# Prompt tokens normalized as rows with a broadcast row of norm weights, first loads in another order, the sample's rstd spread through DRAM

## The chip, the cores and the metric

The kernel runs on one core of a Trainium2 chip. The metric is the device time of one execution in microseconds (us); a lower one is better. The profile is that of one execution, and times in it count from the start of its span.

## The reference

An encoder layer is applied to two batches with the same weights: a prompt of 512 tokens and a sample of 1024 tokens, each token a row of 1024 float32 numbers. Cut to what matters:

```python
def encoder_layer(x, norm_g, w_in, ...):
    h = rmsnorm(x, norm_g)                 # x * rsqrt(mean(x*x) + EPS) * g, row by row
    proj = h @ w_in
    qa, ka, va, za, qb, kb, vb, zb, ga, gb = jnp.split(proj, ...)
    # branch A: 2-D neighbourhood attention, 8 heads; q and k normed by head
    oa = neighbourhood_attention(qa, ka, va, rpb_a) * silu(za)
    # branch B: windowed grouped-query attention with a sink logit and a T5 bias
    ob = window_gqa_attention(qb, kb, vb, t5_table, sink_b) * silu(zb)
    merged = sigmoid(ga) * (oa @ w_o_a) + sigmoid(gb) * (ob @ w_o_b)
    return x + merged @ w_out
```

`norm_g` holds one weight per column, and the factor rsqrt(...), called rstd here, is one number per token.

## The kernel before

Tokens are taken in tiles of 128: four for the prompt, eight for the sample. Everything that a matmul reads is split into a high and a low part (`hh` and `hl` for the normalized tokens, `whi` and `wlo` for weights), and each product is three matmuls: high by high, high by low, low by high. ScalarE writes the high part with a copy, and VectorE or GpSimd subtracts it from the source for the low part. The matmuls want `hh` and `hl` with columns on the partitions and tokens along the row, so tokens have to be transposed.

The work goes in four stages: the prompt's attention, the prompt's dense products, the sample's attention, the sample's dense products. An attention stage has six groups (A0 to A3, B0, B1). For each group four weight pieces of 128x768 are loaded and split (`att_weights`, L568 to L583), and for each token tile 24 matmuls make q, k and v (`project`, L732). The q and k of a tile are then normed (L748 to L784), transposed (L829), and split (L850 to L869); blocks of queries are scored (L902), biased (L937), put through the exponential (L946), scaled (L970 to L978), transposed (L994) and multiplied with v (L1031). The bias of a head is the difference of a mask and a table (L666), where the table comes by way of DRAM: `expand` (L405) writes rows of it out there, and L653 reads them back. Three dense products are taken ahead of their stage as fillers (`fill_gates`, L1430, loads at L1440, tiles `fr`, `fh`, `fl`, PSUM tag `d`).

The order of instructions is made by the class `Flow` (L136). Every operation is recorded with a priority, the engines it may run on, and what it comes behind; `run` (L202) then plays the program through with durations and lags of its own and writes each engine's instructions in the order that comes out. A predecessor in an `after` list is obeyed in that play; on the chip an instruction waits for the data and buffers that it uses.

The prompt's tokens are normalized in `norm_tile` (L504). `rstd` (L432) loads a tile (L438), ScalarE sums its squares (L441), and GpSimd makes the power of -0.5 (L445, L449). TensorE transposes the raw tile in eight blocks (L514). The rstd stands one per partition, while the transposed tokens need it along the row on all partitions, so `spread_rstd` (L454) has ScalarE scale an identity by it (`diag`, L458), TensorE multiply that with a matrix of ones (L463), and ScalarE copy the result out of PSUM (`rb`, L468). `scaled_parts` (L472) then multiplies, 128 columns of the model at a time, the transposed block with the norm weight of its partition (`gx`) and with `rb` (L484), ScalarE copies `hh` (L491) and VectorE or GpSimd subtracts `hl` (L496).

The sample's tokens come transposed from DRAM (`norm_pair`, L537, during the prompt's dense stage). Their rstd is made earlier, tile by tile in the prompt's attention (L1585), with the same `spread_rstd`, into one `rb` of 128x1024.

Loads are issued by SP, one after another in its order. The first stage is opened at L1577; `START` (L32) and `NORM` (L35) are the priorities of the tile loads and of the norms, `FIRST_POOL` (L34) names the weight pieces of the first group whose low part GpSimd has to take, and `setup` (L591) and `expand_ops` (L585) load small tables and expand the bias tables.

## Time and profile before

| what | value |
|---|---|
| time, median of 3 runs (lowest to highest) | 1159.51 us (1157.9 to 1161.04) |
| the profiled execution's own time | 1160.63 us |
| its span, first to last instruction | 1158.8 us |
| TensorE matmuls busy | 1139.2 us |
| VectorE, ScalarE, GpSimd busy | 854.4, 652.2, 325.0 us |
| mean granted TensorE clock | 0.998 |
| bytes moved by DMA | 159.34 MB, mean 138 GB/s |

In the lines of the profile PE is TensorE's matmuls, PEld its weight loads, DVE VectorE, ACT ScalarE, POOL GpSimd and SPq the transfers that SP issues. A line of the timeline has its start in us, its length in us, the engine, the line of the kernel, the operation, what it writes and reads, and in brackets how long the engine stood idle before it and what ended that. A short row of instructions of one kind is one line, with its count. Matmuls overlap: the length of one is the time to its end, and the step from one start to the next is what it costs.

### The profile page before, as it was taken

The numbers are of one execution on the slowest core, as the hardware profiler recorded it, in microseconds if no ns is written. First come the engines' busy times: TensorE is split into PE (matmuls) and PEld (weight loads), VectorE is DVE, ScalarE is ACT, GpSimd is POOL, SyncE is SP. The second block draws the span as 40 slices with busy tenths as digits, with TensorE's granted clock in tenths as the row PEclk, the third lists the DMA queues.
The fourth block names the chain that finished last, engine by engine and source line by source line (L and its number), as shares of the span: only waits on it lengthen the run. The fifth ranks groups of instructions, "written<-read, shape, count | busy, mean of one in ns | idle before, by whom it ended". The sixth has DMA issues, their size and how long they took to land.

```text
span 1158.8 us, 18608 instructions
## 1 busy us (share of the span) xinstructions
PE 1139.2 (98%) x6154; PEld 986.5 (85%) x6154; DVE 854.4 (74%) x1964; ACT 652.2 (56%) x1492; POOL 325.0 (28%) x442
## 2 busy tenths in 40 slices
PE   7999999999999999999999999999999999999998
PEld 6899888888887899999999888888888888788887
DVE  6877888486766468787878888875878555497984
ACT  6966987554434246565768888864534344343320
POOL 4664454100000042434326534440122110031110
PEclk9999999999999999999999999999999999999999
DMA  9842433687786422121212122125767334664072
GB/s 301 302 141 78 130 108 93 152 267 230 232 262 223 151 86 66 33 64 29 71 40 89 38 64 65 37 64 173 245 171 211 115 121 139 216 225 130 28 218 91
DMA packets 124545, 159.34 MB, mean 138 GB/s; under 512 B 28273, under 2 KB 66929, under 8 KB 124449
## 3 DMA queue, kind: packets, MB, share of 16 engines
q1 hardware_dynamic: 124448, 158.16, 44.7%
q8 instruction: 48, 0.79, 0.3%
q14 instruction: 49, 0.39, 0.1%
HBM read 121.40 MB, written 41.44 MB: 141 GB/s over the span
## 4 chain that ended last, share of the span: by engine, by line
PE 84%; ACT 3%; DVE 3%; DMA 2%; issue 1%; POOL 1%; ACTq 0%; DVEq 0%
PE p L732 21%; PE x L1249 9%; PE x L1250 9%; PE x L1248 9%; PE x L1031 4%; PE x L902 4%; PE x L994 4%; PE p L1249 4%; PE p L1248 4%; PE p L1250 4%; PE d L1248 4%; PE d L1250 4%; PE d L1249 4%; PE x L829 1%; DMA ot<-u_d 1%
## 5 line engine op out<-in xcount | busy, mean ns | idle before, releaser
L732 PE MATMUL p<-wlo,hh 128*128 128x384 f32 x384 | 132.0, 344 | 1.6 <-POOL wlo L580 1.6
L732 PE MATMUL p<-whi,hh 128*128 128x384 f32 x384 | 132.9, 347 | 0.6 <-ACT whi L575 0.6
L732 PE MATMUL p<-whi,hl 128*128 128x384 f32 x384 | 132.9, 346 | 0.0
L946 ACT ACTIVATE sb<-sb,mx 128x384 f32<-128x384 f32 (+1 forms) x192 | 107.8, 566 | 21.1 <-DVE mx L937 20.8
L1136 POOL TENSOR_TENSOR wlo<-raw,whi 128x512 fp32r<-128x512 f32 x26 | 37.6, 1445 | 270.9 <-ACT whi L1131 270.8
L1131 ACT ACTIVATE whi<-raw 128x512 fp32r<-128x512 f32 (+1 forms) x140 | 81.2, 590 | 55.1 <-PE x L1249 25.1
L732 PE MATMUL p<-whi,hb 128*128 128x384 f32 x384 | 109.0, 349 | 0.2
L1248 PE MATMUL x<-hh,whi 128*128 128x512 f32 x264 | 102.8, 389 | 1.7 <-ACT hh L1131 1.7
L1249 PE MATMUL x<-hl,whi 128*128 128x512 f32 x264 | 102.8, 389 | 0.2 <-DVE hl L1136 0.2
L1250 PE MATMUL x<-hh,wlo 128*128 128x512 f32 x264 | 102.7, 389 | 0.0
L1005 DVE TENSOR_TENSOR pp<-x,pp 128x512 fp32r<-128x512 f32 (+1 forms) x136 | 82.5, 637 | 22.0 <-ACT pp L1000 21.7
L1136 DVE TENSOR_TENSOR wlo<-raw,whi 128x512 fp32r<-128x512 f32 (+1 forms) x114 | 72.2, 648 | 30.3 <-ACT whi L1131 30.1
L1249 PE MATMUL x<-T,whi 128*128 128x512 f32 x224 | 87.4, 390 | 0.4 <-DVE T L1136 0.2
L1248 PE MATMUL x<-T,whi 128*128 128x512 f32 x224 | 87.3, 390 | 0.1
L1250 PE MATMUL x<-T,wlo 128*128 128x512 f32 x224 | 87.2, 389 | 0.0
L1000 ACT ACTIVATE pp<-x 128x512 fp32r<-128x512 f32 (+1 forms) x136 | 70.8, 562 | 20.8 <-PE x L994 20.0
L767 POOL TENSOR_TENSOR rs_r<-rs_v,mhalf 128x4 f32<-128x4 f32 (+1 forms) x72 | 79.9, 1110 | 5.6
L1031 PE MATMUL x<-pp,v 128*128 128x256 f32 (+1 forms) x368 | 78.5, 325 | 1.4 <-DVE pp L1005 1.4
L732 PEld LDWEIGHTS p<-whi,hh 128*128 128x128 f32 x384 | 72.8, 190 | 1.9 <-ACT whi L575 0.9
L732 PEld LDWEIGHTS p<-wlo,hh 128*128 128x128 f32 x384 | 72.7, 189 | 2.0 <-POOL wlo L580 1.8
L732 PEld LDWEIGHTS p<-whi,hl 128*128 128x128 f32 x384 | 72.7, 189 | 1.8 <-issue 1.5
L732 PEld LDWEIGHTS p<-whi,hb 128*128 128x128 f32 x384 | 69.1, 189 | 3.5 <-ACT hb L633 0.8
(343 smaller groups left out, 2982.3 us busy)
## 6 DMA issues: line engine op xcount, KB each, us to landing
raw<-in_w_g_dram SPq DMA_DIRECT2D x76, 256.0 KB
w<-in_w_att_dram SPq DMA_DIRECT2D x48, 384.0 KB
ot<-o_d SPq DMA_DIRECT2D x36, 256.0 KB
g_d<-C SPq DMA_DIRECT2D x34, 256.0 KB
raw<-in_w_z_dram SPq DMA_DIRECT2D x32, 256.0 KB
raw<-in_w_out_dram SPq DMA_DIRECT2D x32, 256.0 KB
C<-g_d SPq DMA_DIRECT2D x24, 256.0 KB
out_dram<-C SPq DMA_DIRECT2D x23, 256.0 KB
```

Of the source, the lines that this page charges most:

```text
L732: pe.matmul(ps.t[:, :GW], part[u](k), mv.t[:, c], start=k == 0 and m == 0, stop=k == KC - 1 and m == 2,)
L767: lambda e: nc.gpsimd.tensor_tensor(r.t[:, :nn], rv.t[:, :nn], mhalf[:, :nn], op=ALU.pow),
L902: pe.matmul(pss[2 * pair + i].t[:, :width], q.t[rows, u, at : at + P], kv[:, tiles[0] : tiles[-1] + 1 : step], start=n == 0, stop=n == 2,)
L946: act.activation(sb.t[:, :width], sb.t[:, :width], AF.Exp, bias=mx.t[:, i : i + 1], scale=-1.0, accum_out=sm.t[:, i : i + 1],)
L1000: lambda e, pt=pt, pp=pp, nn=nn: act.activation(pp.t[:, 0, :nn], pt.t[:, :nn], AF.Copy),
L1005: lambda e, pt=pt, pp=pp, nn=nn: dve.tensor_tensor(pp.t[:, 1, :nn], pt.t[:, :nn], pp.t[:, 0, :nn].bitcast(F32), op=ALU.subtract),
L1031: pe.matmul(out(), v.t[:, vs], mv(), start=first, stop=last)
L1131: (("act", ACT_(n)),), lambda e: act.activation(hi(), src(), AF.Copy), prio,
L1136: lambda e: engines[e].tensor_tensor(lo(), src(), hi().bitcast(F32), op=ALU.subtract), prio,
L1248: pe.matmul(out, hi.t[:, cs], mh(), start=first and k == 0, stop=False)
L1249: pe.matmul(out, hi.t[:, cs], ml(), start=False, stop=False)
L1250: pe.matmul(out, lo.t[:, cs], mh(), start=False, stop=last and k == len(ws) - 1)
```

## The change

*The norm of the prompt.* The tile is no longer transposed raw. A row of all 1024 norm weights is loaded onto every partition in two halves of 512 columns (`gb`, L1595 of the new code). VectorE multiplies the tile as it lies, tokens on partitions, with its rstd (one per partition) and with that row, 256 columns at a time for tile 0 and 512 for the others (L497). TensorE transposes the products (L507), ScalarE copies `hh` out of PSUM (L512), and VectorE subtracts `hl` out of PSUM (L517). `diag`, the matrix of ones, the L463 matmul and the copy to `rb` are gone for the prompt.

*The sample's rstd.* The eight tiles' rstd are kept as columns of one 128x8 tile `r_s`, which SP writes to DRAM in token order and reads back as a row on all partitions (L1612, L1613), once, in place of eight rounds over ScalarE, TensorE and ScalarE.

*Loads.* Their order at the start is another. Two of the first group's four weight pieces land in a buffer that a bias tile uses later (`place`), so that all four can be asked for at once. Predecessors are given to the loads of tiles 2 and 3, of the bias tables, of the small tables, of the second group's weights, of the sample's tiles and of the fillers' weights (`begun` holds the first matmul of a group and tile). `FIRST_POOL` is empty, so GpSimd is no longer forced on any weight piece.

The diff, cut to its core:

```diff
-FIRST_POOL = (0, 2)
+FIRST_POOL = ()
...
-    def rstd(pool, x, t, prio, load_prio, bufs, after=()):
+    def rstd(pool, x, t, prio, load_prio, bufs, after=(), load_after=(), out=None):
...
+        r = out or val([P, 1], F32, "nr", bufs)
+        rv = lambda: r.t[:, t : t + 1] if out else r.t
+        f.dma(lambda: nc.sync.dma_start(xt.t, x[t * P : (t + 1) * P, :]), 524288, load_prio, new=[xt], after=load_after)
...
-    def spread_rstd(pool, r, t, rb, prio):
...
-    def norm_tile(pool, x, hh, hl, t, prio, load_prio, after=()):
+    def norm_tile(pool, x, gb, gb_ops, hh, hl, t, prio, load_prio, after=(), load_after=()):
+
+        xt, r = rstd(pool, x, t, prio, load_prio, 4, after, load_after)
+        tok = slice(t * P, (t + 1) * P)
+        step, out = 2 if t == 0 else 4, []
+        for k0 in range(0, KC, step):
+            n, cols, ks = step * P, slice(k0 * P, (k0 + step) * P), slice(k0, k0 + step)
+            m = f.op(
+                (("dve", DVE_(n) + 60),),
+                lambda e, cols=cols: dve.scalar_tensor_tensor(
+                    xt.t[:, cols], xt.t[:, cols], r.t, gb.t[:, cols], op0=ALU.mult, op1=ALU.mult
+                ),
+                prio, use=[r], hold=[xt, gb], after=[gb_ops[k0 * P // 512]], port=True,
+            )
+            ps = bank("x")
...
+                    pe.transpose(ps.t[:, i * P : (i + 1) * P], xt.t[:, k * P : (k + 1) * P], ident)
...
+                (("act", ACT_(n, False)),), lambda e, ks=ks, pv=pv: act.activation(hh.t[:, ks, tok], pv(), AF.Copy),
+                prio, use=[ps], hold=[hh],
...
+                lambda e, ks=ks, pv=pv: dve.tensor_tensor(
+                    hl.t[:, ks, tok], pv(), hh.t[:, ks, tok].bitcast(F32), op=ALU.subtract
+                ),
...
-    def att_weights(src, n, prio, engs=("pool", "dve")):
+    def att_weights(src, n, prio, engs=("pool", "dve"), place=None, after=()):
+
+        st, at, new = place or (f.value(wpool, [P, 768], F32, "w32", W32), 0, True)
...
-                    kw = {"new": [ps], "after": [*hs]} if o is None else {"into": [ps], "after": [o]}
+                    kw = {"new": [ps], "after": [*hs, f.begun.get((NT_P, prio - 1)) if nt == NT_P else None]} if o is None else {"into": [ps], "after": [o]}
...
+                    f.begun.setdefault((nt, prio), o)
...
+            early_st = tile_([P, max(2 * at[-1], 4 * GW)], F32, "bias", 2) if gi == 0 and nt == NT_P else None
...
+                    (early_st, 768 * (i - 2), i == 2) if early_st and i > 1 else None,
+                    h_ops[2][:1] if gi == 1 and nt == NT_P else (),
...
-                    dma(lambda raw=raw, src=w_g[m, 2 * br + j]: nc.sync.dma_start(raw.t, src), 262144, prio, new=[raw])
+                    dma(
+                        lambda raw=raw, src=w_g[m, 2 * br + j]: nc.sync.dma_start(raw.t, src), 262144, prio, new=[raw],
+                        after=[f.begun[nt, nb if nt == NT_P else 0]],
+                    )
...
-    f.dma(lambda: nc.sync.dma_start(gx, norm_g), 4096, START[0] + 0.2, into=[gx_v])
+    f.dma(lambda: nc.sync.dma_start(gx, norm_g), 4096, 1, into=[gx_v])
+    gb = f.value(rb_pool, [P, NT_S], F32, "rb", 1)
...
+            lambda i=i: nc.sync.dma_start(gb.t[:, i * 512 : i * 512 + 512], norm_row[i * 512 : i * 512 + 512].partition_broadcast(P)),
+            262144, -7.9 + 0.1 * i, **({"hold": [gb]} if i else {"new": [gb]}),
...
-    setup(norm_p, gp.nb)
-    expand_ops(gp, [max(-1, (h // 2 - 1) * gp.nb) for h in range(8)], h_ops["p"][0][2:3])
+    setup(norm_p, gp.nb, h_ops["p"][3][:1])
+    expand_ops(gp, [max(-1, (h // 2 - 1) * gp.nb) for h in range(8)], [h_ops["p"][t][:1] for t in (1, 3, 3, 3)])
...
-        spread_rstd(norm_p, rstd(norm_p, x_s, t, 6 + 2 * t, 6 + 2 * t, 4)[1], t, rb, 6 + 2 * t)
+        at = 6 + 2 * t
+        rstd(norm_p, x_s, t, at, at, 4, (), [f.begun[NT_P, at - 2]], r_s)
+    o = f.dma(lambda: nc.sync.dma_start(r_d.rearrange("t p -> p t"), r_s.t), 4096, 20, use=[r_s])
+    f.dma(lambda: nc.sync.dma_start(rb.t, r_d.rearrange("t p -> (t p)").partition_broadcast(P)), 524288, 20, new=[rb], after=[o])
```

How the rows move, at three places. The names carry buffer numbers, and the lines of the changed kernel are its own. First SP at the very start, before the change; `xt` are token tiles, `w32` weight pieces, `fr` weights of a filler:

```order
L438 DMA xt_116<-in_x_p_dram 128x1024
L1578 DMA gx_84<-in_norm_g_dram 128x8
L573 DMA w32_119<-in_w_att_dram 128x768
L573 DMA w32_121<-in_w_att_dram 128x768
L438 DMA xt_123<-in_x_p_dram 128x1024
L438 DMA xt_125<-in_x_p_dram 128x1024
L438 DMA xt_127<-in_x_p_dram 128x1024
L593 DMA gcol_72<-in_gains_dram 128x4
L642 DMA mask_138<-in_mask_p_dram 128x512
```

After the change SP starts with these; `rb_119` is the row of norm weights, `bias_126` holds weight pieces 2 and 3, and `raw_257` is the table of head 0:

```order
L440 DMA xt_115<-in_x_p_dram 128x1024
L575 DMA w32_117<-in_w_att_dram 128x768
L1595 DMA rb_119<-in_norm_row_dram 128x512 x2
L575 DMA w32_122<-in_w_att_dram 128x768
L440 DMA xt_124<-in_x_p_dram 128x1024
L575 DMA bias_126<-in_w_att_dram 128x768 x2
L597 DMA gcol_72<-in_gains_dram 128x4
L646 DMA mask_133<-in_mask_p_dram 128x512
L1590 DMA gx_83<-in_norm_g_dram 128x8
L440 DMA xt_175<-in_x_p_dram 128x1024
L440 DMA xt_184<-in_x_p_dram 128x1024
L407 DMA rpb_x512_75<-in_rpb_dram 16x4x768 x4
```

Tiles 2 and 3 (`xt_175`, `xt_184`) have moved behind all four weight pieces and the mask; before, the two first loads for a filler stood ahead of weight pieces 2 and 3, and a sample tile ahead of the second group's weights; now both come behind the second group's weights.

Second TensorE at its start, before the change; `xt_116`, `xt_123` and `xt_125` are tiles 0, 1 and 2, and `p_237` is tile 0's projection:

```order
L514 MATMUL x_130<-ident_66,xt_116 128x128 x4
L514 MATMUL x_140<-ident_66,xt_116 128x128 x4
L463 MATMUL x_167<-diag_159,ones_82 128x128
L514 MATMUL x_175<-ident_66,xt_123 128x128 x4
L514 MATMUL x_183<-ident_66,xt_123 128x128 x4
L514 MATMUL x_203<-ident_66,xt_125 128x128 x4
L463 MATMUL x_223<-diag_209,ones_82 128x128
L514 MATMUL x_226<-ident_66,xt_125 128x128 x4
L732 MATMUL p_237<-whi_149,hh_114 128x384
```

And after it:

```order
L507 MATMUL x_144<-ident_66,xt_115 128x128 x2
L507 MATMUL x_148<-ident_66,xt_115 128x128 x2
L507 MATMUL x_153<-ident_66,xt_115 128x128 x2
L507 MATMUL x_160<-ident_66,xt_115 128x128 x2
L736 MATMUL p_177<-whi_136,hh_113 128x384
```

The transposes of tiles 1 and 2 no longer stand ahead of tile 0's projection: one half of tile 1's comes after 12 of its 24 matmuls, the other half and tile 2's after all 24.

Third VectorE around the q and k of tile 1, before the change; `raw_300` is the table of head 0, `qk_502` the product that TensorE transposes:

```order
L496 TENSOR_TENSOR hl_115<-xt_127,hh_114 128x4x128 x2
L753 TENSOR_REDUCE ss_462<-sq_443 128x4
L777 TENSOR_TENSOR v_448<-p_341,v_448 128x2x64
L580 TENSOR_TENSOR wlo_477<-w32_310,whi_455 128x768
L635 CAST hb_490<-hl_115 128x512
L784 TENSOR_TENSOR qk_502<-p_341,rs_r_483 128x256
```

And after it, with `raw_342` the table of head 1 and `qk_419` tile 1's product:

```order
L758 TENSOR_REDUCE ss_374<-sq_355 128x4
L782 TENSOR_TENSOR v_360<-p_270,v_360 128x2x64
L582 TENSOR_TENSOR wlo_387<-w32_285,whi_363 128x768
L670 TENSOR_TENSOR bias_302<-mask_133,raw_342 128x32x4 x2
L670 TENSOR_TENSOR bias_302<-mask_133,raw_342 128x16x4 x3
L789 TENSOR_TENSOR qk_419<-p_270,rs_r_394 128x256
```

Five operations on a table that comes by way of DRAM now stand ahead of tile 1's product. Between the scores (L902, now L907) and the transposes (L994, now L999) of the prompt's first blocks TensorE's row had fillers and has projections alone now.

More of the change, by code (lines that the diff above doesn't have):

```diff
@@ L448, in rstd @@
         f.op(
[L449 to L450 removed]
+            (("pool", 464),), lambda e: nc.gpsimd.tensor_tensor(rv(), v.t, mhalf[:, :1], op=ALU.pow),
+            prio, use=[v], **({"into": [r]} if out and t else {"new": [r]}),
         )
         return xt, r
[L454 to L470 removed]
     def scaled_parts(xt, src, r, r_op, hh, hl, t, step, prio):
@@ L502, in scaled_parts @@
         return out
-    def norm_tile(pool, x, hh, hl, t, prio, load_prio, after=()):
-        xt, r = rstd(pool, x, t, prio, load_prio, 4, after)
-        pss, reads = [], []
-        for half in range(2):
+    def norm_tile(pool, x, gb, gb_ops, hh, hl, t, prio, load_prio, after=(), load_after=()):
[11 more added lines that the diff above has]
+            )
@@ L509, in norm_tile, with emit @@
             ps = bank("x")
-            def emit(e, half=half, ps=ps):
-                for i in range(4):
-                    k = half * 4 + i
+            def emit(e, k0=k0, ps=ps):
+                for i in range(step):
+                    k = k0 + i
                     pe.transpose(ps.t[:, i * P : (i + 1) * P], xt.t[:, k * P : (k + 1) * P], ident)
-            reads.append(f.op((("pe", 436),), emit, prio, new=[ps], use=[xt]))
-            pss.append(ps)
-        rb = f.value(pool, [P, P], F32, "rb", 2)
@@ L519, in norm_tile @@
-        spread_rstd(pool, r, 0, rb, prio)
-        src = lambda k: ([pss[k // 4]], lambda: pss[k // 4].t[:, k % 4 * P : k % 4 * P + P])
-        xt.writers += reads
-        return [o for ab in scaled_parts(xt, src, lambda: rb.t, rb, hh, hl, t, 2 if t == 0 else 4, prio) for o in ab]
+            f.op((("pe", 109 * step),), emit, prio, new=[ps], after=[m], hold=[xt])
+            pv = lambda ps=ps, n=n: ps.t[:, :n].rearrange("p (k n) -> p k n", n=P)
+            a = f.op(
+                (("act", ACT_(n, False)),), lambda e, ks=ks, pv=pv: act.activation(hh.t[:, ks, tok], pv(), AF.Copy),
+                prio, use=[ps], hold=[hh],
+            )
@@ L524, in norm_tile_t @@
+            b = f.op(
+                (("dve", DVE_(n)),),
+                lambda e, ks=ks, pv=pv: dve.tensor_tensor(
+                    hl.t[:, ks, tok], pv(), hh.t[:, ks, tok].bitcast(F32), op=ALU.subtract
+                ),
+                prio, use=[ps], after=[a], hold=[hh, hl],
+            )
+            out += [a, b]
+        return out
     def norm_tile_t(pool, x_t, rb, hh, hl, t, prio, load_prio):
@@ L597, in setup @@
         )
-        f.dma(lambda: nc.sync.dma_start(raw.t, sink.partition_broadcast(P)), 4096, prio, new=[raw])
+        f.dma(lambda: nc.sync.dma_start(raw.t, sink.partition_broadcast(P)), 4096, prio, new=[raw], after=after)
         sink_v.writers.append(f.op(
```

69 lines of the change are left out of this document (32 added, 37 removed).

## The prediction

> **What bounds the kernel now.** I read the page first: how much of the span TensorE is busy, and in which slices it is not.
>
> ```profile
> PE 1139.2 (98%) x6154; PEld 986.5 (85%) x6154; DVE 854.4 (74%) x1964; ACT 652.2 (56%) x1492; POOL 325.0 (28%) x442
> PE   7999999999999999999999999999999999999998
> ```
>
> TensorE is busy for 1139.2 of 1158.8 us, and only the first and the last slice are below 9. So work saved on another engine counts only where TensorE stands still or runs slowly, and what is taken off TensorE itself counts nearly in full. Second, the list of TensorE's waits (total, times, longest), of which I show those that the start holds:
>
> ```profile
> PE x L514 <- DMA xt<-in_x_p_dram: 5.4, 2, 4.4
> PE x L829 <- DVE qk L784: 2.5, 3, 0.9
> PE p L732 <- POOL wlo L580: 1.6, 1, 1.6
> PE p L732 <- ACT whi L575: 0.6, 1, 0.6
> ```
>
> Third, windows over the start show what waits don't (columns: length, busy time of PE, PEld, DVE, ACT and POOL with counts, granted clock, DMA share, GB/s):
>
> ```profile
> 11.00:14.90 3.90, 3.73 (x24) 3.32 (x23) 3.12 (x13) 3.54 (x9) 1.30 (x3) 1.00 0.94 303
> 14.90:18.30 3.40, 1.15 (x7) 0.72 (x6) 3.40 (x6) 3.38 (x7) 2.88 (x2) 1.00 1.04 314
> 18.30:21.60 3.30, 3.30 (x11) 3.30 (x11) 3.30 (x10) 1.33 (x4) 1.55 (x2) 0.50 0.94 272
> ```
>
> Behind 3.4 us in which PE was busy for 1.15, the granted clock is 0.50 for 3.3 us: only 11 matmuls fit. Fourth, the timeline gives the steps, and the marks to beat:
>
> ```profile
> 4.32 1.06 ACT L441 ACTIVATE junk<-xt 128x1024 bf16<-128x1024 f32 x1 [2.32 <-DMA xt<-in_x_p_dram]
> 5.83 0.57 POOL L449 TENSOR_TENSOR nr<-nv,mhalf 128x1 f32<-128x1 f32 x1
> 8.24 0.96 DVE L580 TENSOR_TENSOR wlo<-w,whi 128x768 fp32r<-128x768 f32 x1 [7.22 <-ACT whi L575]
> 8.64 2.82 PE L514 MATMUL x<-ident,xt 128*128 128x128 f32 x12 [0.96 <-DMA xt<-in_x_p_dram]
> 9.11 1.38 DVE L484 SCALAR_TENSOR_TENSOR xt<-x,gx,rb 128x128 f32<-128x128 f32 x5
> 9.87 1.73 SPq L1440 DMA_DIRECT2D fr<-in_w_g_dram  x2
> 10.41 0.75 DVE L496 TENSOR_TENSOR hl<-xt,hh 128x256 fp32r<-128x256 f32 x2
> 12.41 0.42 PE L732 MATMUL p<-whi,hh 128*128 128x384 f32 x1
> 15.87 2.18 POOL L580 TENSOR_TENSOR wlo<-w,whi 128x768 fp32r<-128x768 f32 x1 [0.27 <-ACT whi L575]
> 16.34 2.26 DVE L496 TENSOR_TENSOR hl<-xt,hh 128x512 fp32r<-128x512 f32 x1
> 18.10 0.56 PE L732 MATMUL p<-wlo,hh 128*128 128x384 f32 x1 [1.60 <-POOL wlo L580]
> 21.66 0.36 PE L732 MATMUL p<-whi,hh 128*128 128x384 f32 x1
> 26.75 0.33 PE L732 MATMUL p<-whi,hh 128*128 128x384 f32 x1
> 30.73 0.34 PE L732 MATMUL p<-whi,hl 128*128 128x384 f32 x1
> 33.94 0.44 PE L829 MATMUL x<-ident,qk 128*128 128x128 f32 x2 [0.80 <-DVE qk L784]
> ```
>
> The first projection starts at 12.41; tile 0 has been issued when tile 1 starts at 21.66, tile 1 when tile 2 starts at 26.75. Undisturbed, 24 matmuls go from 26.75 to one step past 30.73: 0.173 us each. At 15.87 a weight subtraction on GpSimd takes 2.18 us, and a VectorE subtraction beside it 2.26: both late, and TensorE waits for the first.
>
> **The change, part by part.** *Loads.* SP starts eight transfers; the ninth waits for the first to land. The lists of predecessors that the change gives to loads set only their place in SP's row; on the chip an issue is held by the transfer eight before it or by a buffer in use. Tile 0 landed at 4.32, tile 3 by about 11.3 (the second fr issue, inside 9.87 to 11.60, waits for it); between lie two weight pieces and three tiles. Sizes from the list of issues (count, KB each); a prompt tile is as large as one of the sample:
>
> ```profile
> w<-in_w_att_dram SPq DMA_DIRECT2D x48, 384.0 KB
> fr<-in_w_g_dram SPq DMA_DIRECT2D x20, 256.0 KB
> xt<-in_x_s_dram SPq DMA_DIRECT2D x8, 512.0 KB
> rpb_x<-in_rpb_dram SPq DMA_DIRECT2D x16, 192.0 KB
> ```
>
> So 2304 KB came in 6.9 us: 342 GB/s. At that rate, as an estimate, the new row lands weight piece 0 at 5.5, the halves of the norm row at 6.2 and 7.0, piece 1 at 8.1, tile 1 at 9.7, pieces 2 and 3 at 10.8 and 12.0, the mask at 12.7, tiles 2 and 3 at 14.3 and 15.8.
>
> *Tile 0.* Square and power end at 6.40 as before (5.83 + 0.57). Four products of 256 columns follow on VectorE: between 0.375 each (a 256-column subtraction, 10.41 row) and 0.55 (two 128-column products, 1.38/5 each); I take 0.41, near the first, since the fixed part is paid once. With four subtractions of 0.375 and, now that GpSimd takes none, two weight subtractions of 0.96, VectorE has 1.6 + 1.5 + 1.9 = 5.0 us in one row and ends at 11.5. The transposes (2.82/12 = 0.235 each) and ScalarE's copies lie beside that. The first matmul needs only the first columns and can start near 9, the twelfth ends near 12.5, behind the last of these subtractions. Then comes tile 1's first half product (512 columns, about 0.68) and two more weight subtractions, to 14.6, and five matmuls behind the last: 15.5, against 21.66.
>
> *Tile 1.* Most of these 6 us are lost again. Tile 2's transposes stand ahead of tile 1's projection on TensorE; tile 2 lands at 14.3, square and power (1.25 and 0.8) make 16.4, its two products 17.7, the transposes 18.2. So the projection starts at 18.2, and 15 matmuls end at 20.8. What VectorE still has ahead of tile 3's first product:
>
> ```profile
> 22.66 0.41 DVE L753 TENSOR_REDUCE ss<-sq 128x4 f32<-128x256 f32 x1
> 23.59 0.28 DVE L777 TENSOR_TENSOR v<-p,v 128x128 fp32r<-128x128 f32 x1
> L1005 DVE TENSOR_TENSOR pp<-x,pp 128x512 fp32r<-128x512 f32 x112 | 73.9, 685 | 20.2 <-ACT pp L1000 19.9
> ```
>
> From 17.7: three subtractions out of PSUM of 0.685, one reduction and one v, then the product of 0.68: 21.1. Transposes 0.5, the transposes of q and k 0.2, 3 matmuls, 0.5 for the other half, 6 matmuls: tile 2 starts at 23.9, against 26.75. **2.85 us won.**
>
> *Tile 1's q and k.* Their product (0.42 on VectorE) now stands behind five bias operations on the table of head 1. Before, that load behaved so:
>
> ```profile
> 21.58 0.57 SPq L653 DMA_DIRECT2D raw<-rpb_x  x1
> 28.44 0.29 DVE L666 TENSOR_TENSOR bias<-mask,raw 128x128 f32<-128x128 f32 x1 [1.86 <-DMA raw<-rpb_x]
> ```
>
> 6.9 us from issue to use, since the queues were full. After the change its issue waits until head 0's table has been read, near 23.2; with less ahead of it (below), I take 384 KB at 342 GB/s plus as much again, 25.5. VectorE then comes to the product at about 28.1, done 28.6, when TensorE wants it at 28.1: 0.5 us of waiting in place of the 0.8 before 33.94. **0.3 won**; with 6.9 us for the load it would be 4 lost.
>
> *The sample's rstd.* Eight times, and four for the prompt, the two L463 passes leave TensorE:
>
> ```profile
> 53.79 0.38 PE L463 MATMUL x<-diag,ones 128*128 128x128 f32 x2
> 53.93 0.48 PE L1248 MATMUL d<-hh,fh 128*128 128x512 f32 x1
> 54.25 0.39 PE L1249 MATMUL d<-hl,fh 128*128 128x512 f32 x1
> 54.48 0.40 PE L1250 MATMUL d<-hh,fl 128*128 128x512 f32 x1
> ```
>
> They hold it for 0.14, and the next matmul takes 0.32 to its successor in place of 0.23: 0.23 in all, **1.84 us won** for the sample's eight (the prompt's four are in the walk above). In their stead SP writes 1024 single numbers to DRAM and, in a wait at the head of its row, reads them back as a row. Price, from the page's traffic:
>
> ```profile
> q1 hardware_dynamic: 124448, 158.16, 44.7%
> ```
>
> 0.447 x 16 x 1158.8 / 124448 = 0.067 us of an engine per packet, of 1.3 KB on average; 1024 packets over 16 engines make 4.3 us, with the landing some 6. Behind the waiting issue stand weights that only the sample's attention uses and half a bias table of the last group, for which ScalarE then waits; TensorE has some 5 us of matmuls in between. I take 0, bounds 0 and 2, and the sample's rb itself is needed only when sample tiles are scaled, in the prompt's dense phase. [...]
>
> *Other edits.* The early weight pieces in the bias buffer cost nothing new: the buffer is free until head 0's table comes. Fillers (d matmuls) come later, the same number; their cover is discussed below. ScalarE loses 24 small operations.
>
> *The clock.* From 18.10 to 21.66 eleven matmuls took 0.324 us each in place of 0.173, 1.6 us in all, and the walk counts that as gone. After the change TensorE is busy for some 2.0 of the 3.4 us before 18.3 (0.6 to 15.5 and three groups of transposes of 0.45), between the 1.15 that was punished and the 3.73 of 3.90 that was not. [...]
>
> **Sum.** 2.85 + 0.3 + 1.84 = 5.0 us. The profiled execution took 1160.63 (span 1158.8 and 1.8 around it), which gives 1155.6; it lay 1.1 above the median of the three runs, 1159.51. Against that median: **1154.5**. Bounds: each us by which loads come later than 342 GB/s beyond 0.3 us of slack is one us less, since tile 2's landing is on the path; 410 GB/s, or less waiting behind 60 us, gives up to 3 us more: 1151.5 to 1156.
>
> **The rivals.**
> *The clock halves again* in the gap before 18.2. For it: 2.0 of 3.4 us busy is nearer to 1.15. Against: the idleness comes in pieces under 1 us. 1.6 us back: 1156.1.
> *The table of head 1 is late*, as before the change, and TensorE waits at the q and k of tile 1: 4 us lost in place of 0.3 won, 1158.8. Against it: six expansions of 192 KB stand ahead of it, not thirteen, and no sample tile (512 KB) and no fr loads (two of 256 KB).
> *The gain is given back*: later stages run at a pace set by loads or VectorE, not by TensorE. For it, VectorE at 74%; against, the 98% of TensorE. About 1159.
> *Slower: the softmax is uncovered.* Before, fillers stand between the scores and the transposes of the first attention blocks; now projections alone do. The chain is:
>
> ```profile
> 98.40 0.42 DVE L937 CUSTOM_DVE_ANT_0 sb<-x,bias 128x256 f32<-128x256 f32 x1
> 101.09 0.81 PE L994 MATMUL x<-ident,sb 128*128 128x128 f32 x4
> ```
>
> 2.7 us when VectorE is free, and in the new row 3.1 to 5.2 us of matmuls, at the steps above, stand between the scores and the first transposes of a pair of blocks. It decides when VectorE or ScalarE are 1.1 us late at each of the eight block pairs: 8.8 lost, 1163.3.
>
> **How the numbers follow.** Forecast 0.54; clock 0.14; late table 0.12; given back 0.10; slower 0.10. A measurement of this kernel can tell about 0.3%, 3.5 us, from no change: faster means under 1156.0. The forecast is all faster, the clock about one in three: 0.58. The late table, the given-back gain and the rest of the clock: 0.32. Slower 0.10. The range goes from 1151.5 over the clock, the late table and the given-back gain to 1160; it leaves out the slower case.
>
> **What would show it.** Right: no L463; first projection before 10.5, tile 1 at about 18.2 and tile 2 near 24; no clock of 0.50 in the first 30 us; a wait under 1 us at the q and k of tile 1; no GpSimd wlo in the first 20 us and no VectorE subtraction above 1 us there. Wrong: tile 2 landing after 15.5, TensorE waits at L999 after each L907, or a busy share of TensorE under 98% behind 40 us.

## The result, and the profile after

The changed kernel takes 1170.7 us, the median of four runs (1170.51 to 1174.36); the kernel before took 1160.28 (four runs, 1157.9 to 1162.63). The ratio is 1.0097, with a 95% interval of 1.0068 to 1.0127: about 10 us slower, where 5 us faster was forecast. The profiled execution has a span of 1168.7 us, 9.9 more than before.

The page first: busy time, and the 40 slices of 29.2 us.

```profile
PE 1137.3 (97%) x6130; PEld 985.3 (84%) x6130; DVE 854.1 (73%) x1934; ACT 653.3 (56%) x1484; POOL 323.0 (28%) x433
PE   6899969999999999999999999999999999999998
```

TensorE is busy for 1.9 us less than before and the span is 9.9 us longer, so the loss is idle time, and slow clock, which counts as busy. Beside the start (6), two slices stand out, 29 to 58 us (8) and 146 to 175 us (6). TensorE's waits name what ended them:

```profile
PE x L507 <- DVE xt L497: 8.6, 2, 7.9
PE p L736 <- ACT hb L637: 8.5, 1, 8.5
PE x L999 <- DVE sb L983: 2.4, 2, 2.1
PE x L834 <- DVE nsink L604: 1.1, 1, 1.1
```

The first is the start, before the first transposes. The second is new and a single wait. Its timeline (start, length, engine and line; the wait before it in brackets):

```profile
145.38 0.39 SPq L1612 DMA_DIRECT2D r_d<-r_s  x1
146.10 0.45 SPq L683 DMA_DIRECT2D raw<-line_d  x1
146.65 1.29 SPq L1064 DMA_DIRECT2D o_d<-ot__2106  x2
156.83 0.34 SPq L1613 DMA_DIRECT2D rb<-r_d  x1
158.33 0.51 SPq L683 DMA_DIRECT2D raw<-line_d  x1
162.80 0.61 ACT L637 ACTIVATE bias<-raw 128x384 f32<-128x384 f32 x1 [9.94 <-DMA raw<-line_d]
164.45 0.69 PE L736 MATMUL p<-whi,hb 128*128 128x384 f32 x1 [8.48 <-ACT hb L637]
```

The store of the 1024 single numbers is issued at 145.38, and its readback leaves SP's row at 156.83, 11.45 us later. Behind the readback stands the second half of a bias table (L683, 158.33). ScalarE waits 9.94 us for that half, and next in ScalarE's row stands the copy hb that TensorE needs. Windows over the same stretch (length, busy time of PE, PEld, DVE, ACT, POOL, granted clock, DMA share, GB/s):

```profile
149.00:156.00 7.00, 6.97 (x41) 6.02 (x39) 4.80 (x18) 3.71 (x13) 5.08 (x6) 1.00 0.00 1
156.00:164.40 8.40, 0.00 (x0) 0.00 (x0) 0.00 (x0) 1.60 (x3) 0.00 (x0) 0.78 0.60 201
164.40:171.00 6.60, 5.50 (x16) 4.72 (x17) 4.77 (x9) 5.29 (x11) 2.95 (x2) 0.50 0.41 140
```

For seven microseconds the DMA engines move nothing, though a store is outstanding; TensorE still has work. Then everything stands. When TensorE starts again its clock is 0.50 for another 6.6 us, in which 5.5 us of matmuls do the work of 2.75. The place costs 8.5 + 1.0 (the next q and k) + 2.75 = 12.3 us, more than the whole loss.

The start, and the marks that the prediction set:

```profile
7.37 0.88 DVE L497 SCALAR_TENSOR_TENSOR xt<-xt,nr,rb 128x256 f32<-128x256 f32 x2 [6.52 <-DMA rb<-in_norm_row_dram]
9.18 0.88 DVE L497 SCALAR_TENSOR_TENSOR xt<-xt,nr,rb 128x256 f32<-128x256 f32 x2 [0.93 <-DMA rb<-in_norm_row_dram]
10.48 0.67 PE L736 MATMUL p<-whi,hh 128*128 128x384 f32 x1
16.42 0.60 ACT L512 ACTIVATE hh<-x 128x512 fp32r<-128x512 f32 x1 [2.19 <-PE x L507]
16.82 0.52 PE L736 MATMUL p<-whi,hl 128*128 128x384 f32 x1
16.92 1.05 ACT L443 ACTIVATE junk<-xt 128x1024 bf16<-128x1024 f32 x1
17.14 0.43 PE L736 MATMUL p<-whi,hh 128*128 128x384 f32 x1
21.06 0.43 PE L736 MATMUL p<-whi,hh 128*128 128x384 f32 x1
26.48 0.33 PE L736 MATMUL p<-whi,hh 128*128 128x384 f32 x1
```

Tile 1's projection starts at 21.06 (21.66 before) and tile 2's, 24 matmuls later, at 26.48 (26.75 before): 0.27 us won in place of 2.85. The ScalarE lines are its copy of tile 1's first half (16.42), which waits for that half's transposes, and tile 2's sum of squares (16.92), which stands behind the copy. Third, the slice before 58 us:

```profile
51.16 0.42 DVE L789 TENSOR_TENSOR qk<-p,rs_r 128x256 f32<-128x256 f32 x1 [1.86 <-POOL rs_r L772]
51.48 0.72 POOL L1049 TENSOR_TENSOR ot__676<-ot__676 64x256 f32<-64x256 f32 x1
51.62 3.88 DVE L1053 TENSOR_TENSOR ot__668<-ot__668 64x256 f32<-64x256 f32 x1
52.17 0.55 POOL L451 TENSOR_TENSOR r_s<-nv,mhalf 128x1 f32<-128x1 f32 x1
52.69 2.52 POOL L1145 TENSOR_TENSOR fl<-fr,fh 128x512 fp32r<-128x512 f32 x2
58.62 0.81 PE L999 MATMUL x<-ident,sb 128*128 128x128 f32 x4 [2.14 <-DVE sb L983]
```

A VectorE addition that takes 0.42 us elsewhere takes 3.88, and ends at 55.50, just behind GpSimd's unbroken row of instructions (52.69 + 2.52 = 55.21). The softmax behind it is late, and TensorE waits 2.14 us for it at 58.62.

How far each kernel is behind the one before at a given moment: I count the matmuls issued up to then, each at its step at full clock (0.173 us for 384 columns, 0.23 for 512, 0.09 for a transpose), and look up when the kernel before had issued as many. The passes of L463 do not count as work. Since some records are missing, and work stands in another order, it is good to about 1 us. Each line but the first two has the row store; `old prompt` is the kernel before with the spread alone.

```
us behind the kernel before   at 30    48    60   150   200   300   600
changed                        -0.3   0.8   4.3   2.3  13.8  14.9  12.3
late readback                  -1.4  -0.2   5.1   3.5  11.1  12.1   9.8
row store                      -1.2  -0.4   4.2   1.6   2.0   2.1  -1.0
old prompt, row store           0.2  -0.4  -0.5  -1.5  -1.1  -0.8  -3.3
rows alone, row store           1.5   0.7   0.9   2.3   2.9   3.9   1.9
order alone, row store         -0.8   1.9   4.7   2.0   3.6   3.9   1.4
filler subtractions on VectorE -1.1  -1.1   2.4   3.1   3.8   4.5   1.7
tables on VectorE              -0.8   3.1   3.9   1.0   1.5   1.8   0.9
warm start                     -2.0  -2.1   2.7  -0.5   0.2   0.8   0.8
```

The first line has two steps: some 4 us between 48 and 60, and some 12 between 150 and 200. The other lines are experiments, told below.

### The profile page after: what moved, and what is told of

Same layout as the page of the kernel before. It is cut to its first block, busy times and chain, and to the rows that moved or that the text cites. A ratio compares the mean times of both kernels' runs of the same rounds, so it can differ in the third digit from the quotient of the medians.

```text
span 1168.7 us, 18486 instructions
## 1 busy us (share of the span) xinstructions
PE 1137.3 (97%) x6130; PEld 985.3 (84%) x6130; DVE 854.1 (73%) x1934; ACT 653.3 (56%) x1484; POOL 323.0 (28%) x433
## 4 chain that ended last, share of the span: by engine, by line
PE 87%; DMA 5%; ACT 3%; DVE 2%; POOL 1%; issue 1%; SPq 1%; ACTq 0%; POOLq 0%; DVEq 0%
PE p L736 21%; PE x L1258 9%; PE x L1257 9%; PE x L1259 9%; PE x L1036 5%; PE p L1258 4%; PE p L1257 4%; PE p L1259 4%; PE x L999 4%; PE x L907 4%; PE d L1257 4%; PE d L1259 4%; PE d L1258 4%; PE x L834 2%; DMA r_d<-r_s 1%
## 5 line engine op out<-in xcount | busy, mean ns | idle before, releaser
L1145 POOL TENSOR_TENSOR wlo<-raw,whi 128x512 fp32r<-128x512 f32 x28 | 41.6, 1485 | 304.1 <-ACT whi L1140 146.5
```

The lines of the kernel that those rows point to most:

```text
L1145: lambda e: engines[e].tensor_tensor(lo(), src(), hi().bitcast(F32), op=ALU.subtract), prio,
```

## Experiments

The theory after reading the trace: the store of single numbers holds SP, and with it a table, and costs 12 us; the rest of the change is worth about 2. Its rival: the time is lost in the first 60 us, and the stall only takes up slack that later stages would have used. Ratios are to the kernel before, with 95% intervals.

**Late readback.** Only the place of the readback in SP's row changes.

```diff
-    f.dma(lambda: nc.sync.dma_start(rb.t, ...), 524288, 20, new=[rb], after=[o])
+    f.dma(lambda: nc.sync.dma_start(rb.t, ...), 524288, 20, new=[rb], after=[o, f.begun[NT_P, 23]])
```

> Store and readback of the sample's rstd are as in the changed kernel; only the readback stands 12 rows later in SP's row, behind the loads and stores of the next 20 us, and every other engine has the same row. Theory 'held issue': SP stood 8.9 us at the readback for the store, a bias table behind it came late, and TensorE paid 8.5 us of idleness, 1.0 us at the next q and k, and 5.6 us of work at half clock (2.8): 12.3 in all. Then this kernel takes the changed kernel's 1170.7 less 12.3 = 1158.4, a ratio of 0.998 to the kernel before, with no TensorE wait above 2 us between 100 and 200 us and no clock of 0.50 there. Rival 'packets': the 1024 four-byte packets themselves hold up the tables in the queues; then the table still lands late, a wait of some 5 us or more stays, and the ratio is above 1.003. Rival 'start': the lost time lies in the first 60 us and the stall only takes up slack of later stages; then the ratio stays near 1.009.

Measured: 1167.07 us, ratio 1.0056 (1.0037 to 1.0075). TensorE's wait is shorter and not gone:

```profile
PE p L736 <- ACT hb L637: 4.9, 1, 4.9
```

Windows of this kernel, columns as above:

```profile
149.00:152.00 3.00, 3.00 (x17) 2.65 (x16) 3.00 (x13) 3.00 (x9) 2.92 (x3) 1.00 1.00 30
152.00:155.00 3.00, 3.00 (x19) 2.75 (x18) 2.33 (x10) 1.02 (x6) 2.83 (x5) 1.00 0.61 33
155.00:158.00 3.00, 1.75 (x13) 1.34 (x11) 0.24 (x1) 0.00 (x0) 0.02 (x1) 1.00 0.39 27
158.00:160.00 2.00, 0.00 (x0) 0.00 (x0) 0.00 (x0) 0.02 (x1) 0.00 (x0) 1.00 0.99 311
```

SP no longer waits and issues table and weights by 150, but they come at 27 to 33 GB/s until 158, then at 311. So my theory was half of it: the store also slows the loads that are issued behind it, until some 12 us after its own issue (146.0). It does not hold everything: half a table issued at 146.58, and two small stores at 147.2, were through by 149.5 at their usual pace. The rival "packets" is right that the store holds up loads in the queues; "start" falls. The packets themselves are not what takes long: in the trace of the changed kernel all 1024 are recorded between 146.0 and 147.0, 7 ns each, and the readback leaves 9.8 us after the last of them. Why such a store lands so late stays open.

**Eight stores** of 128 numbers, each as soon as its tile's rstd is ready.

```diff
-    o = f.dma(lambda: nc.sync.dma_start(r_d.rearrange("t p -> p t"), r_s.t), 4096, 20, use=[r_s])
+        o = f.dma(lambda t=t: nc.sync.dma_start(r_d[t], r_s.t[:, t : t + 1]), 512, at, hold=[r_s], after=r_s.writers[-1:])
```

> The readback keeps its place in SP's row, behind the last of eight stores of 128 numbers, each issued when its tile's rstd is ready; TensorE's row is the same. If the landing time of a store grows with its packets (about 11 us from issue for 1024, so 1.4 for 128 and a fixed part of about 2), SP waits under 3 us at the readback, TensorE's stall near 156 us is under 2 us, and the ratio to the kernel before is 0.998 to 1.000. Rival: a store of single numbers lands late whatever its size; then SP again waits 8 to 9 us, TensorE idles about 8 us, and the ratio stays near 1.009.

Measured: 1202.03 us, 1.036 (1.034 to 1.038): far slower still. The last store and the readback in SP's row, then TensorE's waits of the first 300 us:

```profile
177.80 0.33 SPq L1612 DMA_DIRECT2D r_d<-r_s  x1
185.55 0.33 SPq L1613 DMA_DIRECT2D rb<-r_d  x1
```

```profile
PE x L1036 <- DVE pp L1010: 14.4, 2, 9.6
PE x L999 <- POOL sb L981: 6.3, 2, 5.8
PE p L736 <- ACT hb L637: 5.5, 1, 5.5
```

128 numbers take 7.75 us from issue to readback, 1024 took 11.45. An eighth of the numbers saves a third of the time, and now there are eight stores to hold up what stands behind them: after the first (issued at 56.20) the loads come at 23 to 51 GB/s from 58 to 66 us, and TensorE stands for 9.6 us until 71.81. I had expected 1.4 us and, as an estimate, a fixed 2 (SP's longest wait for a store of g_d in the changed kernel is 2.2); that was wrong.

**Row store.** TensorE turns the 128x8 numbers into 8 rows of 512 bytes.

```diff
+    f.op((("pe", 109),), lambda e: pe.transpose(rp.t[: gs.nb, :P], r_s.t, ident), 20, new=[rp], use=[r_s])
+    f.op((("act", ACT_(P, False)),), lambda e: act.activation(rt.t, rp.t[: gs.nb, :P], AF.Copy), 20, new=[rt], use=[rp])
-    o = f.dma(lambda: nc.sync.dma_start(r_d.rearrange("t p -> p t"), r_s.t), 4096, 20, use=[r_s])
+    o = f.dma(lambda: nc.sync.dma_start(r_d, rt.t), 4096, 20, use=[rt])
```

> TensorE turns the 128x8 rstd into 8x128 first, so that the store has 8 rows of 512 bytes in place of 1024 single numbers; store and readback stand at the same place in SP's row. Theory 'held issue' with the size of the packets as cause: the store lands about 2 us after its issue, SP waits 1 to 3 us, the TensorE stall near 156 us goes, ratio 0.998 to 1.000. Rival: any store with a readback through DRAM takes some 10 us; then SP waits 8 to 9 us and the ratio is about 1.009.

```profile
154.36 0.30 SPq L1615 DMA_DIRECT2D r_d<-r_t  x1
155.78 0.54 SPq L1616 DMA_DIRECT2D rb<-r_d  x1
```

Measured: 1159.76 us, 0.9992 (0.998 to 1.0005), and 1.42 us from issue to readback. One transposition takes the whole loss away: 1.0097 / 0.9992 is 1.05%, some 12 us, the 12.3 of the stall.

**Old spread** in the changed kernel: diagonal, two passes and copy per sample tile, nothing through DRAM.

```diff
-        rstd(norm_p, x_s, t, at, at, 4, (), [f.begun[NT_P, at - 2]], r_s)
+        spread_rstd(norm_p, rstd(norm_p, x_s, t, at, at, 4, (), [f.begun[NT_P, at - 2]])[1], t, rb, at)
```

> The changed kernel with the sample's rstd spread as before the change: a diagonal on ScalarE, two passes on TensorE and a copy, eight times, and nothing through DRAM; all else as changed. By 'held issue' the 12.3 us stall goes and eight times 0.23 = 1.8 us of TensorE come back, so 1170.7 - 12.3 + 1.8 = 1160.2, a ratio of 1.000, and 1.8 us more than the kernel with the late readback. By the rival 'start' the ratio is 1.009. If the two passes cost nothing in truth, this kernel and the one with the late readback take the same time.

Measured: 1163.13 us, 1.003 (1.0019 to 1.0041): 3.4 us over the row store by the medians, where eight passes by themselves are 1.8. The stall is gone here too, but this kernel has only the prompt part of the change, and that by itself makes it 3.5 us slower (2.2 to 4.8). That was not in the theory.

**The kernel before with the spread alone**: first with the store of single numbers, then with the row store (the edits above on the kernel before).

> The kernel before the change with one part of the change: the sample's eight rstd columns go to DRAM in one store of 1024 single numbers and come back as a row, in place of eight diagonals and pairs of passes; the prompt is normalized as before. The store stands near 57 us, two rows ahead of the readback; behind these stand a bias table and the weights of the second and third group. If such a store holds the queues for 8 to 11 us wherever it stands, tables and weights come late and TensorE waits some 3 to 9 us near 70 us, less the 1.8 us of passes: ratio 1.002 to 1.006. If the cost belongs to the place where the change put it (the last group's table), the ratio is 0.997.

> As the last, with the store as 8 rows of 512 bytes, turned on TensorE first; the prompt is normalized as before. This is the spread's gain by itself: 1.8 us by the prediction, a ratio of 0.998; 3.4 to 4.4 us, 0.9965, if the difference between the changed kernel with a row store (0.9992) and with the old spread (1.003) is all the spread's. If the prompt part of the change gains the 3.15 us that the prediction gave it, this kernel is 3 us slower than the changed kernel with a row store; if the prompt part loses as much near 50 us as it wins at the start, the two are equal or this one is faster.

With single numbers: 1165.62 us, 1.0037 (1.002 to 1.0053). Store and readback, at another place of the program:

```profile
61.21 0.38 SPq L1591 DMA_DIRECT2D r_d<-r_s  x1
72.01 0.32 SPq L1592 DMA_DIRECT2D rb<-r_d  x1
```

```profile
PE x L905 <- DVE kt L858: 7.7, 1, 7.7
```

10.8 us again, and a wait of 7.7: the cost goes with the store, not with the place. With the row store: 1156.19 us, **0.9945** (0.9927 to 0.9962), the fastest kernel of the study, faster than both, and by more than I had expected. It is 2.0 us ahead at 120 to 130 us and, by the table, 1.5 at 150 and 1.1 at 200, about what the passes promise (1.84), and 3.3 at 600. Part of the rest is a TensorE wait on ScalarE's hh between 300 and 400 us, 1.7 us in the kernel before and 0.4 here. The change with the same row store is 0.9992: beside this kernel its prompt part costs about 5 us (5.4 by the ratios, 3.6 by the medians), and alone, in the kernel with the old spread, 3.5.

**Packets of 32 bytes.** The last kernel and one more store, near 62 us, that nothing reads: the same 1024 numbers as 128 packets of 32 bytes.

```diff
+    f.dma(lambda: nc.sync.dma_start(r_x, r_s.t), 4096, 20, use=[r_s])
```

> The kernel before with the spread through a row store (0.9945), and one more store of the same 1024 numbers near 61 us that nothing reads, as 128 packets of 32 bytes. In the kernel before with the store of 1024 packets of 4 bytes at this place, TensorE waited 7.7 us near 75 us and the ratio was 1.0037. If it is the single numbers that hold the queues, 32 bytes a packet cost little: ratio 0.9945 to 0.996, no TensorE wait above 2 us between 60 and 90 us. If every store of packets far under 512 bytes holds them, whatever the count (128 packets of 4 bytes did too), the wait is 5 to 8 us and the ratio 1.000 to 1.004.

Measured: 1156.82 us, 0.9963 (0.9948 to 0.9978), just above the range expected. TensorE's only wait between 58 and 95 us:

```profile
PE x L833 <- DVE qk L788: 0.8, 1, 0.8
```

Nothing reads this store, so SP does not wait for it, and its landing is not seen. What it does to the queues is: the next load in SP's row is the same filler load in both kernels, issued at 63.15 here and at 62.46 behind the single numbers. Windows over its packets, first here, then there:

```profile
64.00:65.00 1.00, 1.00 (x8) 1.00 (x7) 1.00 (x4) 0.51 (x3) 1.00 (x3) 1.00 0.52 180
66.00:73.00 7.00, 4.52 (x30) 3.77 (x28) 1.76 (x3) 1.38 (x5) 1.35 (x1) 1.00 0.21 29
```

180 GB/s against 29: 128 packets of 32 bytes hold no load up; 128 packets of 4 bytes did (the eight stores).

**What in the prompt part costs 5 us.** Seven kernels, all with the row store. First the two that take GpSimd's two filler subtractions, and the gate on the fillers' loads, out of the changed kernel:

```diff
             b = f.op(
-                any_tt(n),
+                engs or any_tt(n),
...
+                        engs=(("dve", DVE_(nh)),) if nt == NT_P else None,
```

> The changed kernel with the row store, and the subtractions of the filler weights on VectorE alone. In the four kernels with the changed start so far, a VectorE addition of 64x256 at 51 to 52 us takes 3.85 to 3.88 us in place of 0.42, ending as GpSimd's unbroken row of four instructions ends, whose last two are these subtractions (2.5 us); the softmax behind it is 3.4 us late and the work on TensorE falls from level to 4 us behind the kernel before between 48 and 60 us. Theory 'GpSimd holds VectorE': without the two the addition ends some 2.5 us sooner, TensorE is about 2 us less behind at 60 us, ratio 0.9975. Rival 'late table': the whole block is late because the bias table behind the broadcasts and expansions came 5 us late, and TensorE has no fillers there; then the loss at 60 us stays at 4 and the ratio at 0.999.

```diff
-                        after=[f.begun[nt, nb if nt == NT_P else 0]],
+                        after=[f.begun[nt, 0]],
```

> The changed kernel with the row store, and the loads of the filler weights let free from the first projection on, not from the second group on, so that fillers can stand in the first attention blocks as before the change. If the loss between 48 and 60 us is want of fillers, TensorE falls less far behind there (2 us or more recovered) and the ratio is 0.9975 or lower. If the loss is GpSimd's row or the late table, the early loads only take from the tables' share of the queues: ratio 0.999 to 1.002.

Filler subtractions on VectorE: 0.9991 (0.9977 to 1.0006). The addition takes its usual time:

```profile
51.74 0.42 DVE L1053 TENSOR_TENSOR ot__668<-ot__668 64x256 f32<-64x256 f32 x1
```

TensorE is 1.8 us less behind at 60 us (2.4 for 4.2), so GpSimd did hold VectorE; but by 150 it has given that back, and the time is the same. Fillers let free: 1.0019 (1.0004 to 1.0034), slower. By the same count the fall between 48 and 60 us is 2.0 us here and 4.6 without the edit, so fillers do cover part of it; but tile 2's projection starts at 28.34, for 25.54, and 4 us more are lost between 150 and 200. Want of early fillers alone is not the cause of the time.

Next the two halves of the prompt part: rows alone on the kernel before (with the row store; the edit is cut to its core), and the new order of loads with the old normalization; and the changed kernel without the rule that orders a tile's projection behind the start of the one before.

```diff
-    f.dma(lambda: nc.sync.dma_start(gx, norm_g), 4096, START[0] + 0.2, into=[gx_v])
+    f.dma(lambda: nc.sync.dma_start(gx, norm_g), 4096, 1, into=[gx_v])
+    gb = f.value(rb_pool, [P, NT_S], F32, "rb", 1)
...
-        h_ops["p"][t] = norm_tile(norm_p, x_p, *h_p, t, ...)
+        h_ops["p"][t] = norm_tile(norm_p, x_p, gb, gb_ops, *h_p, t, ...)
```

> The kernel before with the spread through a row store (0.9945) and the prompt's tiles normalized as rows with the broadcast norm row loaded ahead; the order of all other loads, the gates and the early weight buffer stay as before the change. If the 5.4 us that the prompt part of the change costs come from its load order and gates, this is at 0.9945 or below, down to 0.993 if the start wins 2 us here. If they come from the rows themselves (a first product that waits for the norm row, TensorE cold at its first projections), it is at 0.998 or above.

The second takes the same lines the other way, in the changed kernel with the row store:

> The complement: load order, gates, early weight buffer and row store as in the changed kernel with the row store (0.9992), and the prompt's tiles normalized as before the change, with the diagonal and two passes per tile. If order and gates cost the 5.4 us, this is at 0.999 or a little above, and TensorE falls 4 to 5 us back between 48 and 65 us as in all kernels with that order. If the rows cost it, it is near 0.9945 and does not fall back there.

```diff
-                    kw = {"new": [ps], "after": [*hs, f.begun.get((NT_P, prio - 1)) if nt == NT_P else None]} if o is None else {"into": [ps], "after": [o]}
+                    kw = {"new": [ps], "after": [*hs]} if o is None else {"into": [ps], "after": [o]}
```

> The changed kernel with the row store, without the rule that a tile's projection in a group is ordered behind the start of the tile's before it. If that rule is what leaves the first attention blocks without work beside them, TensorE falls back by less than 2 us between 48 and 65 us and the ratio is 0.996 or lower; if not, 0.998 to 1.000 and the same fall.

Rows alone: 1.0006 (0.9991 to 1.0021). Order alone: 1.0 (0.9987 to 1.0013), with the fall before 60 us. Both: 0.9992. Each half costs as much as the two together, so the cost is no sum of parts. Without the rule: 0.9989 (0.9976 to 1.0002), the same fall (0.7 us behind at 48, 5.7 at 60); it is not the cause.

Last, the two causes that the trace names for the start and for the wait at 48 to 51 us, each taken out of the changed kernel with the row store:

```diff
-                                (("dve", DVE_(n // 2)), ("pool", POOL_(n // 2))), emit, prio,
+                                (("dve", DVE_(n // 2)),) if nt == NT_P else (("dve", DVE_(n // 2)), ("pool", POOL_(n // 2))), emit, prio,
```

> The changed kernel with the row store (0.9992), and the prompt's bias tables of the first four groups made on VectorE alone. In the kernels with the changed start, GpSimd waited 5 to 7 us for the fourth table's load, then made six pieces of it in 2.9 us, and the rstd of q and k came 2.2 to 2.5 us late behind them; TensorE waited so long at 48 to 51 us and then ran at half clock for 3.3 us. Theory 'tables on GpSimd': with the pieces off GpSimd the wait and the half clock go, and TensorE is 3 us less behind at 60 us; if nothing gives it back, ratio 0.9965. Rival 'given back', as when the filler subtractions left GpSimd: the mark at 60 us improves and the time does not, ratio 0.998 to 1.000.

```diff
+    for i in range(10):
+        wp = bank("x")
...
+            for j in range(4):
+                pe.transpose(wp.t[:, j * P : (j + 1) * P], ident, ident)
+
+        f.op((("pe", 436),), emit, -30, new=[wp])
```

> The changed kernel with the row store, and 40 transposes of the identity that nothing reads, ahead of the first tile's, while TensorE stands idle for the norm row. In the changed kernel the matmuls of the first projection follow each other at 0.32 us until 17.1 us and at 0.173 after. If that is the clock of an engine that had stood still, the first projection here runs at 0.173, tile 1's projection starts 1 to 2 us before 21.06 and the mark at 30 us is 1 us or more ahead; ratio 0.9975 to 0.999. If loads or VectorE set the start in any case, the steps are closer and tile 1 still starts near 21; ratio 0.999.

Tables on VectorE: 0.9992 (0.9978 to 1.0006). The wait at 48 to 51 is gone, and another has come, on a small table's load, with half clock behind it:

```profile
34.08 1.86 PE L614 MATMUL x<-hot_sb,t_sb 32*8 32x512 f32 x2 [3.40 <-DMA hot_sb<-in_t_hot_dram]
```

Warm start: 1.0011 (0.9998 to 1.0024). Tile 1 starts at 19.52, 1.54 us earlier than in the changed kernel and 0.65 earlier than in the one with the row store (20.17), and the q and k of a later tile are late all the same:

```profile
19.52 0.42 PE L736 MATMUL p<-whi,hh 128*128 128x384 f32 x1
49.96 0.41 PE L834 MATMUL x<-ident,qk 128*128 128x128 f32 x2 [2.63 <-DVE qk L789]
```

Three local cures (filler subtractions, tables, warm start) worked where they were applied, and none made the kernel faster than the 0.9992 it had; with the warm start it is, if anything, slower.

## Why the prediction was wrong, by its steps

*The sample's rstd, the read and write through DRAM: "I take 0, bounds 0 and 2".* This is the step that failed. It was worked out as 1024 packets at 0.067 us on 16 engines, "with the landing some 6", against "some 5 us of matmuls in between". Issue to readback was 11.45 us. TensorE had more cover than I gave it, it ran dry 10.6 us after the issue (156.0), but the table came through ScalarE 6 us after the readback had left, and half clock followed (0.50 for 6.6 us): 12.3 us. The 0.067 us was the price of packets of 1.3 KB carried over to packets of 4 bytes. The packets turned out cheaper than that, all recorded within 1 us; what cost was the landing, some 10 us behind the last of them, and the loads held meanwhile. The sum had no term of that size, and its upper bound was not a bound: no row showed such a store. What the runs show of the size: a store of 128 packets of 32 bytes held up no load (180 GB/s over its packets), while of the eight stores of 128 packets of 4 bytes the first held the loads behind it (23 to 51 GB/s) and the last landed after 7.75 us.

*The passes that leave TensorE: 1.84 us.* Right in size, as far as the count tells: TensorE is 1.1 to 2.0 us ahead between 120 and 200 us when only the spread changes, and in the changed kernel the row store is 2.0 us ahead of the old spread at 200. The kernel before with it gains 6.4 us by its ratio (4.4 to 8.5). So about 4 us more come from elsewhere, of which the trace names 1.3, the shorter wait on hh.

*The start: 2.85 us.* Measured 0.27 in the profiled execution; in the eight profiles with this start tile 2's projection begins at 25.54 to 26.69, for 26.75 before. No GpSimd subtraction of weights stood in the first 20 us and none on VectorE took over 1 us, as forecast. As I had it, an issue of SP was held by the transfer eight before it: the eleventh waited 0.9 us for the third, the first half of the norm row, and the twelfth 1.6 for the fourth, the other half. The order of steps was right and each was later. The norm row's halves came at 7.37 and 9.18, for 6.2 and 7.0 at 342 GB/s. The first projection started at 10.48, within the mark of 10.5, but its matmuls followed each other at 0.32 us (16.82 to 17.14) until about 17.1 and at 0.17 from 17.42 on, and I had costed them all at 0.17. So its first twelve were through at 15.33, for 12.5. That, and not tile 2's landing as I had it, set what came next: ScalarE stood at the copy of tile 1's first half, whose transposes come behind these twelve, and began tile 2's squares at 16.92, for 14.3. Tile 1 started at 21.06 for 18.2.

How much of these 2.9 us is the step of 0.32? The warm start brings tile 1 forward by 1.54, but 0.88 of that it has at its first projection already (9.60), mostly because the norm row's second half came sooner there (8.41 for 9.18). From there to tile 1 it takes 9.92 us, and the eight profiles without it take 9.99 to 10.69: the steps of 0.32 account for 0.1 to 0.8 us. The rest begins with the norm row, whose halves were 1.2 and 2.2 late.

*The clock.* "No clock of 0.50 in the first 30 us" came true in the column and was of no use: the column shows 1.00 in the very stretch in which matmuls step at 0.32. They hang on what TensorE did before: in the kernel with the warm start it is busy for 6.66 of the 7 us up to 8.00, and the first projection's matmuls step at 0.17 (11.16 to 11.33). The column could not tell: the trace's clock record has its first entry at 17.35 us (14.70 with the row store, 6.15 with the warm start), and the column reads 1.00 where the record has none.

*Tile 1's q and k: 0.3 won.* The wait was 1.1 us (the list puts it down to nsink, the small VectorE instruction behind the product) for 0.80 before: 0.3 lost. The step that I worried about held: the table of head 1 came in time, and its five operations ended at 30.18. But then VectorE waited 1.19 us, until 31.36, for GpSimd's rstd of q and k, which the walk did not have.

*The rival "softmax uncovered", 0.10.* It named the right mechanism, a first block without fillers whose transposes wait for VectorE, and the wrong size: 1.1 us at each of eight pairs. In the changed kernel it happened at one pair, with 2.14 us of wait there and some 4 us lost in all between 48 and 60. I had seen a subtraction on GpSimd and one on VectorE both run long at 16 us (2.18 for 1.85, 2.26 for 0.68) and used it only as something the change removes; here the new order brings the like back with other operands (3.88 for 0.42).

*The sum.* The change is three things. Put on the kernel before in this order, the spread is worth -6.4 us, its single numbers +12 and the prompt part +5; with the prompt part first, they are +3.5 for it, -4.4 for the spread and +12 for the single numbers. The forecast had -1.8 for the spread, 0 for the single numbers and -3.2 for the prompt part.

What stays open: why the prompt part costs 5 us. The places are known (small tables and bias tables whose loads come late; GpSimd's instructions ahead of the rstd of q and k; half clock behind the waits in some of the profiles), and taking one out showed each where it stood. But with one removed another took its place, and each half alone costs as much as both. That the planner's order for the kernel before simply happened to fit the chip well is likely, and only argued.

## What to carry to other kernels

Price a DMA by the size of its packets and by the time until it has landed, which the packets' own times do not show (all 1024 within 1 us here, and the readback 9.8 us after the last of them); and when no row shows that size, do not call the nearest row a bound. A small result that must cross partitions through DRAM should be turned on chip first, so that it leaves in rows, here 8 of 512 bytes: one transposition saved 12 us. Ask of every slow transfer what is queued behind it, both in the issuing engine's row and in the DMA queues, since moving the wait alone took the stall from 8.5 us to 4.9 and no further. And a local gain near the start of a planned kernel counts only if the mark is still ahead some hundred microseconds later.

## What the hardware showed that I had not expected

- The readback behind a store of single 4-byte numbers is issued 7.75 us (128 of them) to 11.45 us (1024) after the store, though the 1024 packets are all recorded within 1 us. Behind the 1024, loads came at 27 to 33 GB/s until 12 us after the store's issue, and at 311 then. With the same numbers in 8 rows of 512 bytes it was 1.42 us, and as 128 packets of 32 bytes they held up no load (180 GB/s over their packets).
- While such a store is outstanding and nothing is queued, the DMA share reads 0.00 for 7 us. Quiet queues do not mean that a store has landed.
- A VectorE addition of 64x256 took 3.88 us in place of 0.42, until GpSimd's row of four instructions had ended (55.50 and 55.21); taking two of these off GpSimd gave 0.42 back.
- Some waits of TensorE were paid again in clock. Two cases, windows with TensorE's busy time and the granted clock behind it: the kernel with the row store, after a wait of 2.2 us that ended at 51.35, and the one with the tables on VectorE, after the 3.40 us that ended at 34.08 (all engines).

```profile
52.00:54.00 2.00, 2.00 (x9) 0.56 0.44 174
54.00:56.00 2.00, 2.00 (x9) 0.59 0.00 0
```

```profile
34.00:37.40 3.40, 3.33 (x8) 1.66 (x9) 1.16 (x3) 0.63 (x2) 0.09 (x1) 0.50 1.04 354
```

Nine matmuls in the first window, at steps of 0.32 us in place of 0.173; the changed kernel's profile has 14 in the same window. There a stall's price was the wait and half of what ran in the 3.4 us or more behind it. Not every wait costs this: behind 2.52 us at the same place in the kernel with the old spread, which ended at 51.72, the granted clock stayed at 1.00.
